# A hybrid layer: state-space outputs on quarter tiles, modulations moved into the state-space stage, TensorE order pinned there

## The chip, the core and the metric

The kernel runs on one core of a Trainium2 chip. The metric is the device time of one execution, in microseconds (us). A core has a matrix engine, TensorE (PE in the profile, its weight loads PEld), and VectorE (DVE), ScalarE (ACT) and GpSimd (POOL) beside it; SyncE (SP) only issues DMAs here, and its queue is in order. PSUM, where matmuls write, has eight banks of 128 partitions x 512 numbers of four bytes.

## The reference

One layer over 512 latent tokens with 256 context tokens in front, width 1024: an adaptive norm, one input projection, then two branches (a bidirectional state-space scan with 32 groups of 64 complex states, and attention with 8 query heads on 2 key heads), merged by gates, and a gated FFN with a short convolution. The modulations (shift, scale and gate vectors from `c`) are a vector times a 1024 x 6144 matrix.

```python
def _modulate(h, shift, scale):
    return h * (1.0 + scale) + shift
...
def _s5_readout(s_re, s_im, c_re, c_im):
    y = (jnp.einsum('blgn,gpn->blgp', s_re, c_re.astype(jnp.float32))
         - jnp.einsum('blgn,gpn->blgp', s_im, c_im.astype(jnp.float32)))
    return y.reshape(y.shape[0], y.shape[1], SSM_DIM)
...
    y_lat = u_lat.astype(jnp.float32) * d
    for direction in range(N_DIRECTIONS):
        sl_re, sl_im, sc_re, sc_im = _s5_direction(
            uc, ul, lam_re[direction], lam_im[direction], log_dt[direction],
            b_re[direction], b_im[direction], reverse=(direction == 1))
        y_lat = y_lat + _s5_readout(sl_re, sl_im, c_re[direction], c_im[direction])
...
def _merge_branches(attn_tok, ssm_tok, g, w_attn_br, w_glu, w_out):
    p_attn = attn_tok @ w_attn_br
    glu_a, glu_b = jnp.split(jax.nn.gelu(ssm_tok) @ w_glu, 2, axis=-1)
    p_ssm = glu_a * jax.nn.sigmoid(glu_b)
    g_attn, g_ssm = jnp.split(g, N_BRANCHES, axis=-1)
    return (jax.nn.sigmoid(g_attn) * p_attn + jax.nn.sigmoid(g_ssm) * p_ssm) @ w_out
...
        mod = jax.nn.silu(c) @ w_mod[layer] + b_mod[layer]
        sh1, sc1, g1, sh2, sc2, g2 = jnp.split(mod[:, None, :], N_MOD, axis=-1)
        h = _modulate(_rmsnorm(x, norm1_w[layer]), sh1, sc1)
        q, k, v, u, g = jnp.split(h @ w_in_l, (Q_END, K_END, V_END, U_END), axis=-1)
        attn_tok = _tokens(_gqa_sweep(q, jnp.concatenate([kc, k], axis=2),
                                      jnp.concatenate([vc, v], axis=2)))
        y_ssm, y_ssm_c = _s5_bidirectional(...)
        x_mix = _merge_branches(attn_tok, y_ssm, g, w_attn_br[layer], w_glu[layer], w_out[layer])
        x = x + g1 * x_mix
        h2 = _modulate(_rmsnorm(x, norm2_w[layer]), sh2, sc2)
        x = x + g2 * _conv_ffn(h2, w_up[layer], conv_w[layer], conv_b[layer], w_down[layer])
    return _rmsnorm(x, final_norm_w)
```

## The kernel before

All arithmetic is in four-byte numbers. A large product is made of three PE passes: operands are split into a high and a low part, and `mm3` (L127) adds high x high, low x high, high x low. `weight` (L136) loads a weight tile in pieces of 128x512 (`wr`, three buffers), ScalarE casts the high part `wh` (L133) and GpSimd subtracts for the low part `wl` (L134); both have two buffers. The stages, in us of the profiled execution:

- 0 to 82: norms, the modulations that the first norm needs (`wmA`), and the projection u for the scan, which goes to DRAM by block (`ud`, L418).
- 82 to 112: keys; lag matrices of block 0 (`s5_lags`, L462) and its tables (`turn`, L484).
- 112.5 to 286: the state-space stage, four blocks `s` of eight groups each in two halves `h`. `s5_build` makes W and H of a block with twelve DVE operations; `s5_lags` multiplies them on PE into `kps`, and turns the result through DRAM (`ldr`) into `tp`; `s5_drive` (L498) transposes W (`gps`) and multiplies it with u into two banks `gp`, of which it uses columns 0 to 4 x 96 of 512; `s5_half` (L521) multiplies by tables and scans on DVE, and then makes the outputs `y2` on PE: per group one full matmul with `tp` and u (L125) and four on 64 rows of the array with H and the states `q1` (L558), each streaming 64 columns. `s5_end` (L561) copies y2 and turns it through DRAM: one issue to `yd`, eight back into `y`. Beside this run v (`values_all`, six tiles `vp`) and twelve gate tiles (`gate_tile`, tiles `proj`, tanh on ACT): `beside(i)` writes them between the halves.
- 286 to 318: the gelu of y, and the first queries and scores. 318 to 500: the head loop, eight heads of four query blocks each: scores `sc`, softmax on DVE and ACT, transposes `tps` of P, value matmuls `po`, and between these, as filler, matmuls of the query two heads on (`query`) or of a gate, and of `glu`. In this loop stand the 16 remaining modulations, two per head (at j 0 and 3; turned at j 1 and 4): `mods_load` (L685) asks for one 1 MB tile `wm`, `mods_row` (L690) multiplies it with `c` on 32 columns of the array at a time, ScalarE copies the row to `tg` (L694), `mods_turn` (L697) turns it with two one-column matmuls and DVE adds the bias.
- 500 to 605: both branches' output projections. 605 to 990: the FFN, `up` and `down`.

PSUM banks come by tag: `a` and `b` two banks each, `s` two pairs. `vp`, `proj` in the stage, and `mods` have tag `a`; `gps` and `kps` have `b`; `gp`, `y2` and `sc` have `s`. What sets the order: in the head loop it is that of the code (`pinned`, L120: each matmul of `mm` is tied to the one before it). In the state-space stage it is not tied, and a scheduler chooses among what is written there. A `f32` matmul that is not of the split kind is two records in the profile: the eight of a modulation row are x16.

## Time and profile before

| | us |
|---|---|
| median of 3 runs | 993.87 |
| lowest and highest | 991.27, 996.55 |
| the profiled execution | 992.33 |
| its span in the profile | 990.3 |
| PE busy | 927.7 |
| state-space stage (112.5 to 286), PE busy in it | 173.5, 158.93 |
| head loop (318 to 500), PE busy in it | 182.0, 181.37 |

The span runs from the first to the last instruction; the execution's own time has some 2 us around it. A matmul's record overlaps the next one's, so a mean duration is longer than the distance from one to the next; the chain of work that ended last gives the distance. The windows give the clock that was granted to PE as a share of 2.4 GHz, as a mean over the stretch.

### The profile page before, as it was taken

How to read it: one execution, taken by the hardware profiler on the slowest of the kernel's cores; microseconds unless marked ns; L12 is line 12 of the kernel's file. 1: busy time of each engine (PE TensorE's matmuls, PEld its weight loads, DVE VectorE, ACT ScalarE, POOL GpSimd, SP SyncE). 2: the span in 40 equal slices, each digit the busy share in tenths (PEclk: the TensorE clock that was granted, in tenths of full speed). 3: DMA queues.
4: the chain of work that ended last, by engine and by line, in shares of the span. 5: the costliest groups of instructions: out<-in, count | busy, mean ns of one | idle time of the engine just before them, and what ended most of it. 6: DMA issues, size and time to landing. Idle time of an engine off the chain costs nothing.

```text
span 990.3 us, 14447 instructions
## 1 busy us (share of the span) xinstructions
PE 927.7 (94%) x5522; PEld 762.1 (77%) x5522; DVE 500.1 (51%) x957; ACT 406.0 (41%) x749; POOL 370.9 (37%) x282
## 2 busy tenths in 40 slices
PE   3978987999998999999999999999999999999996
PEld 1757776787886787777778898888888888888886
DVE  8497595769666666667433564423233332300103
ACT  7325432343264444444432343534443444432322
POOL 2242131532331221122235430655656555544553
PEclk9999998988999999999999999999999999999998
DMA  9516314151343233333313530232222323233332
GB/s 367 221 58 193 75 49 123 49 144 49 99 136 107 103 113 126 128 128 124 110 65 128 189 111 1 85 103 89 97 96 87 104 86 103 85 101 96 96 106 85
DMA packets 59443, 109.25 MB, mean 110 GB/s; under 512 B 10608, under 2 KB 23664, under 8 KB 55664
## 3 DMA queue, kind: packets, MB, share of 16 engines
q1 hardware_dynamic: 59376, 108.35, 33.6%
q8 instruction: 43, 0.70, 0.3%
q14 instruction: 24, 0.20, 0.1%
HBM read 102.06 MB, written 6.26 MB: 109 GB/s over the span
## 4 chain that ended last, share of the span: by engine, by line
PE 76%; DVE 8%; issue 4%; DMA 4%; POOL 3%; ACT 3%; SPq 2%; DVEq 0%; ACTq 0%; POOLq 0%
PE up L125 25%; PE down L125 12%; PE proj L125 10%; PE po L125 6%; PE glu L125 5%; PE sc L125 3%; PE pab L125 3%; POOL wl L134 3%; PE tps L805 2%; DMA wr<-wo 2%; PE mods L366 2%; PE y L558 1%; PE gp L517 1%; PE kp L125 1%; DVE tg L228 1%
## 5 line engine op out<-in xcount | busy, mean ns | idle before, releaser
L134 POOL TENSOR_TENSOR wl<-wr,wh 128x512 fp32r<-128x512 f32 x226 | 318.7, 1430 | 576.3 <-ACT wh L133 565.8
L125 PE MATMUL up<-t,wh 128*128 128x512 f32 (+1 forms) x768 | 225.5, 377 | 1.6 <-DVE t L933 0.9
L133 ACT CAST wh<-wr 128x512 fp32r<-128x512 f32 x226 | 127.8, 609 | 131.0 <-PE down L125 40.5
L125 PEld LDWEIGHTS up<-t,wh 128*128 128x128 f32 x768 | 140.0, 188 | 32.0 <-DVE t L933 2.4
L125 PE MATMUL up<-t,wl 128*128 128x512 f32 (+1 forms) x384 | 144.7, 377 | 0.0
L125 PE MATMUL proj<-h,wh 128*128 128x512 f32 x384 | 130.6, 408 | 3.0 <-DVE g L134 2.1
L125 PEld LDWEIGHTS proj<-h,wh 128*128 128x128 f32 x384 | 74.3, 194 | 17.9 <-ACT g L133 2.2
L125 PEld LDWEIGHTS up<-t,wl 128*128 128x128 f32 x384 | 72.2, 188 | 14.7
L125 PE MATMUL proj<-h,wl 128*128 128x512 f32 x192 | 78.1, 407 | 2.5 <-POOL wl L134 2.5
L967 DVE SCALAR_TENSOR_TENSOR zc<-up,pv,zc 128x511 f32<-128x511 f32 x44 | 33.0, 750 | 88.3 <-ACT zc L966 88.3
L966 ACT ACTIVATE zc<-up,pv 128x512 f32<-128x512 f32 x44 | 34.2, 777 | 74.9 <-PE up L125 74.9
L998 DVE SCALAR_TENSOR_TENSOR x<-down,mods,x 128x512 f32<-128x512 f32 (+1 forms) x9 | 6.2, 691 | 90.7 <-PE down L125 90.7
L125 PEld LDWEIGHTS proj<-h,wl 128*128 128x128 f32 x192 | 37.4, 195 | 10.0 <-POOL wl L134 3.1
L125 PE MATMUL glu<-w,wh 128*128 128x512 f32 x128 | 44.2, 406 | 0.0
L134 DVE TENSOR_TENSOR ptl<-tps,pth 128x512 fp32r<-128x512 f32 x48 | 33.1, 689 | 16.6 <-ACT pth L133 16.1
L133 ACT CAST pth<-tps 128x512 fp32r<-128x512 f32 x48 | 28.2, 587 | 32.1 <-PE tps L805 32.1
L793 DVE TENSOR_REDUCE sc<-sc 128x1 f32<-128x768 f32 x32 | 30.7, 961 | 19.7 <-PE sc L125 19.7
L125 PE MATMUL sc<-g,qh 128*128 128x256 f32 (+1 forms) x128 | 37.6, 347 | 0.0
L125 PE MATMUL down<-h,wh 128*128 128x512 f32 x112 | 35.6, 389 | 0.0
L968 DVE SCALAR_TENSOR_TENSOR zc<-up,pv,zc 128x511 f32<-128x511 f32 x44 | 33.0, 750 | 1.5
L106 ACT ACTIVATE P<-sc,nb,rq 128x768 f32<-128x768 f32 x32 | 31.7, 993 | 4.8 <-DVE nb L794 3.1
L125 PE MATMUL po<-pth,g 128*128 128x512 f32 x96 | 32.4, 418 | 0.6 <-ACT pth L133 0.6
(286 smaller groups left out, 1763.3 us busy)
## 6 DMA issues: line engine op xcount, KB each, us to landing
wr<-wup SPq DMA_DIRECT2D x88, 256.0 KB
wm<-wmB SPq DMA_DIRECT2D x16, 1024.0 KB
wr<-wdn SPq DMA_DIRECT2D x40, 256.0 KB
x<-x SPq DMA_DIRECT2D x4, 1024.0 KB
g<-wmA SPq DMA_DIRECT2D x4, 1024.0 KB
w<-wmA SPq DMA_DIRECT2D x4, 1024.0 KB
wr<-wgs SPq DMA_DIRECT2D x16, 256.0 KB
wr<-wga SPq DMA_DIRECT2D x16, 256.0 KB
```

What stands on the lines that cost most here:

```text
L106: i = A.activation(*a, **k).ins
L125: pe(T.matmul(ps, l, r, start=start, stop=stop).ins)
L133: A.copy(hi, src)
L134: eng.tensor_tensor(lo, src, f(hi), op=OP.subtract)
L228: eng.tensor_tensor(o, a, b, op=op)
L366: pe(T.matmul(ps[c:c + 32, 0:n], l, r, start=j < 4, stop=j >= len(terms) - 4, tile_position=(0, c)).ins)
L517: T.matmul(gp[64 * g:64 * g + 64, ri, o:o + NC], gt[:, 2 * d + ri, 64 * g:64 * g + 64], u[:, 2 * k + g, c], start=True, stop=True, tile_po ...
L793: V.tensor_reduce(mx, sv, axis=AX.X, op=OP.max)
L805: pe(T.transpose(tps[:, 128 * b:128 * b + 128], Ps[h][b][:, 128 * j:128 * j + 128], ident).ins)
L966: A.activation(z, ps, AF.Identity, scale=cw[1], bias=pv[:, PV_CB + i:PV_CB + i + 1])
L967: V.scalar_tensor_tensor(z[:, 1:512], ps[:, 0:511], cw[0], z[:, 1:512], op0=OP.mult, op1=OP.add)
L968: V.scalar_tensor_tensor(z[:, 0:511], ps[:, 1:512], cw[2], z[:, 0:511], op0=OP.mult, op1=OP.add)
```

## The change

- The outputs of a half block are made after the scans by `s5_out`: u and the states `q1` are now the stationary operands and `tp` and H stream, 128 columns each; every matmul of the states uses a quarter of the array (64 rows x 64 columns), the one with u a half (64 columns). A pair of halves (k2, g) goes to partitions 64 x (g xor k2) of bank k2; they write into columns 384 to 512 of the `gp` banks of the same half's drive, which the drive leaves free. So `y2` is gone.
- `s5_end` turns y on PE against the identity (16 matmuls a block, quarter tiles) in a bank `yt` of tag `b`; the way through DRAM is gone. u is written to DRAM in an order in which one DMA per block (`s5_u`) reads it, eight before. On the host, columns of `w_u` and rows of `w_glu` are put in the matching order.
- All 16 modulations leave the head loop. They are made in the stage, each as two half rows (`wm` of 512 KB, two buffers); the row's copy goes to a buffer `bb`, and the bias is added by two ScalarE activations.
- PE's order in the stage is pinned. Generators yield after pieces of a few matmuls, and `weave(one, two, n, m)` takes n steps of the one with m of the other spread between them. `filler` is the list of six v tiles, twelve gates and, between their steps, the modulations; `steps(fill, ..)`, `GAP` and F0 to F3 say how much of it goes where.
- The low part of v is subtracted from a second copy `vr` that ScalarE makes, not from the bank. The tiles `p` have two buffers, three before, and z shares the one of p2.

```diff
+GAP, F0, F1, F2, F3, WM = 2, 8, 13, 5, 2, 2
...
     def s5_u(s):
-        u = tz([8, NC + NL], "u", 2)
-        for t in range(TC):
-            S.dma_start(u[16 * t:16 * t + 16], us_[s][:, t].rearrange("(j q) c -> q j c", j=8))
-        return u
-
+        us[s] = tz([8, NC + NL], "u", 2)
+        S.dma_start(us[s], us_[s].rearrange("t (q j) c -> (t q) j c", j=8))
...
+    def weave(one, two, n, m):
+
+        j = 0
+        for i in range(n):
+            next(one, None)
+            while j * n < (i + 1) * m:
+                next(two, None)
+                j += 1
+        run(one)
...
-        blocks[s] = W, H, tp, s5_u(s)
+        blocks[s] = W, H, tp, us[s]
...
+        for _ in range(GAP):
+            next(fill, None)
+            yield
...
         tt(q1[:, 0], q1[:, 0], q2[:, 1], OP.add)
         tt(q1[:, 1], q1[:, 1], q2[:, 0], OP.subtract)
-        for k2 in range(2):
-            k = 2 * h + k2
-            o = slice(NL * k, NL * k + NL)
-            for g in range(2):
-                mm(y2[:, g, o], tp[:, 2 * k + g], u[:, 2 * k + g, NC:NC + NL], True, False)
-            for d in range(2):
-                for ri in range(2):
-                    for g in range(2):
-                        pa = slice(64 * g, 64 * g + 64)
-                        T.matmul(y2[:, g, o], H[pa, ri, 2 * k + d], q1[pa, ri, 2 * k2 + d], start=False,
-                                 stop=d + ri == 2, tile_position=(64 * g, 0))
-
-    def s5_end(s, y2):
-        ys = t2()
-        A.copy(ys.rearrange("p (k g c) -> p g k c", k=4, g=2), y2[:, :, 0:4 * NL].rearrange("p g (k c) -> p g k c", k=4))
-        yd = dram.tile([128, 8, NL], F32, tag="yd", name="yd", bufs=4)
-        S.dma_start(yd, ys.rearrange("p (j c) -> p j c", j=8))
+        outs[s, h] = q1
+        yield
+
+    def s5_out(s, h, ys):
+
+        W, H, tp, u = blocks[s]
+        gp, q1 = drives.pop((s, h)), outs.pop((s, h))
+        four = [(k2, g, 2 * h + k2, slice(64 * (g ^ k2), 64 * (g ^ k2) + 64)) for k2 in range(2) for g in range(2)]
+        o = slice(4 * NC, 512)
+        for k2, g, k, px in four:
+            pe(T.matmul(gp[px, k2, o], u[:, 2 * k + g, NC:NC + NL], tp[:, 2 * k + g], start=True, stop=False,
+                        tile_position=(0, px.start)).ins)
+        for d in range(2):
+            for ri in range(2):
+                for k2, g, k, px in four:
+                    pa = slice(64 * g, 64 * g + 64)
+                    pe(T.matmul(gp[px, k2, o], q1[pa, ri, 2 * k2 + d], H[pa, ri, 2 * k + d], start=False, stop=d + ri == 2,
+                                tile_position=(64 * g, px.start)).ins)
+        A.copy(ys.rearrange("p (t b k l) -> p b k t l", t=TC, b=2, k=2)[:, :, h],
+               gp[:, :, o].rearrange("p b (t l) -> p b t l", t=TC))
+
+    def s5_end(s, ys):
+
+        yt = bank("yt", "b")
         for t in range(TC):
-            S.dma_start(y[:, s, NL * t:NL * t + NL], yd[16 * t:16 * t + 16].rearrange("p j c -> j p c"))
-
-    s5_build(0)
+            for px in (slice(0, 64), slice(64, 128)):
+                pe(T.matmul(yt[px, NL * t:NL * t + NL], ys[px, 64 * t:64 * t + 64], ident[px, px],
+                            start=True, stop=True, tile_position=(px.start, px.start)).ins)
+        A.copy(y[:, s], yt)
+
+    run(s5_build(0))
...
+    def v_tile(j, w):
+        ps = bank("vp")[:, :256]
+        for k in range(KT):
+            if j < 2:
+                st_ = (ch[:, k, 128 * j:128 * j + 128], cl[:, k, 128 * j:128 * j + 128])
+            else:
+                st_ = (hh[k][:, 128 * j - 256:128 * j - 128], hl[k][:, 128 * j - 256:128 * j - 128])
+            mm3(ps, st_, (w[k // 4][0][:, k % 4], w[k // 4][1][:, k % 4]), k == 0, k == KT - 1)
+            if k == KT - 1:
+                A.copy(vh[:, j], ps)
+                raw = tz([256], "vr")
+                A.copy(raw, ps)
+                V.tensor_tensor(vl[:, j], raw, f(vh[:, j]), op=OP.subtract)
+            if k % 2:
+                yield
+
+    ms, ga = [], []
+
+    def gate_w(i):
+        return weight(io["wgs" if i < 8 else "wga"][i % 8], [KT, 128])
+
+    def gate_of(o, w, tag):
+
+        ps = bank("proj", tag)
+        for k in range(KT):
+            mm3(ps, (w[0][:, k], w[1][:, k]), (hh[k], hl[k]), k == 0, k == KT - 1)
+            if k == KT - 1:
+                act(o, ps, AF.Tanh, scale=0.5)
+            yield
+
+
+    mods = tl([4, KT], "mods")
+    pieces = []
+
+    def mods_load():
+        p = len(pieces)
+        if p < 32:
+            wm = tz([4, 256], "wm", WM)
+            nosync(S.dma_start(wm, io["wmB"][p // 2, :, 4 * (p % 2):4 * (p % 2) + 4]).ins, last[0])
+            pieces.append(wm)
+
+    def mods_all():
+
+        yield
+        for i in range(16):
+            ps = bank("mods")
+            for p in range(2):
+                wm = pieces[2 * i + p]
+                for j in range(4):
+                    pe(T.matmul(ps[32 * j:32 * j + 32, 0:256], cz[:, 4 * p + j], wm[:, j], start=p == 0, stop=p == 1,
+                                tile_position=(0, 32 * j)).ins)
+                mods_load()
+                if p == 0:
+                    yield
+            row = tz([256], "bb", 2)
+            A.copy(row, ps[:, 0:256])
+            yield
+            for t in range(2):
+                mm(ps[:, 256 + t:257 + t], row[:, 128 * t:128 * t + 128], sel[:, 0:1], True, True)
+            o = PV_BMOD + 16 + 2 * i
+            for t in range(2):
+                acts["run"].append(A.activation(mods.rearrange("p v k -> p (v k)")[:, 2 * i + t:2 * i + t + 1],
+                                                ps[:, 256 + t:257 + t], AF.Identity, bias=pv[:, o + t:o + t + 1]).ins)
+            yield
+
+    def filler():
+        mod = mods_all()
         wv_ = [weight(io["wv"][i], [4, 256]) for i in range(2)]
+        jobs = [("v", j) for j in range(6)] + [("g", i) for i in range(8 + NGA)]
+        w = wv_
+        for n, (kind, i) in enumerate(jobs):
+            if kind == "v":
+                gen = v_tile(i, wv_)
+            else:
+                if i == 0:
+                    ms.extend(rows("x8", F32))
+                if i == 8:
+                    ga.extend(rows("c8", F32))
+                gen = gate_of((ms + ga)[i], w, "a")
+            if n + 1 < len(jobs) and jobs[n + 1][0] == "g":
+                w = gate_w(jobs[n + 1][1])
+            m = 0
+            for _ in gen:
+                m += 1
+                yield
+                if n < 16 and m in ((1, 2, 4) if kind == "v" else (2, 5, 8)):
+                    next(mod, None)
+        for _ in mod:
+            yield
...
+    fill = filler()
+    for _ in range(WM):
+        mods_load()
+    pinned[0] = True
+    run(s5_drive(0, 0))
+    for s in range(4):
+        ys = t2()
+        if s < 3:
+            s5_u(s + 1)
+
+        weave(s5_half(s, 0), chain(s5_drive(s, 1), fill), 8, 6 + F0)
+        s5_out(s, 0, ys)
+        if s < 3:
+            weave(chain(turn(2 * s + 2), s5_build(s + 1)), fill, 15, F1)
+            weave(chain(s5_half(s, 1), turn(2 * s + 3)), chain(s5_drive(s + 1, 0), s5_lags(s + 1), fill), 8, 9 + F2)
         else:
+            weave(s5_half(s, 1), fill, 8, F0)
+        s5_out(s, 1, ys)
+        steps(fill, F3)
+        s5_end(s, ys)
+    run(fill)
+    pinned[0] = False
...
-            if j in (1, 4):
-                mods_turn(*turning)
             if j < 4 and h + 1 < HEADS:
                 scores(h + 1, j)
-            if j in (0, 3):
-                turning = mods_row(*wm)
-                if wm[0] < 15:
-                    wm = mods_load(wm[0] + 1)
...
```

TensorE, the outputs of a half block. Rows are line, operation, out<-in and shape; the numbers behind `h` tell apart the buffers of the norm's output. Before (`y` is the pair of banks y2):

```order
L125 MATMUL proj<-h_265,wh 128x512
L125 MATMUL proj<-h_264,wh 128x512
L125 MATMUL proj<-h_264,wl 128x512
L558 MATMUL y_1550<-tg,w_1304 128x64 x8
L125 MATMUL y_1550<-u,tp 128x64 x2
L558 MATMUL y_1550<-tg,w_1304 128x64 x8
L125 MATMUL y_1550<-u,tp 128x64 x2
L125 MATMUL proj<-h_266,wh 128x512
```

And now:

```order
L127 MATMUL proj<-h_263,wl 128x512
L127 MATMUL proj<-h_265,wh 128x512
L596 MATMUL gp<-tp,u 64x128 x4
L602 MATMUL gp<-w_1299,tg 64x128 x16
L127 MATMUL proj<-h_264,wh 128x512
L127 MATMUL proj<-h_264,wl 128x512
L127 MATMUL proj<-h_266,wh 128x512
L726 MATMUL mods<-wm,cz 32x256 x4
```

The group has 20 matmuls as before, of 128 columns each and not 64, and the half row of a modulation stands close by.

TensorE, the step from one gate tile to the next (the first rows are the end of a tile, where `h_264` and `h_266` are used; a tile begins with `h_263`). Before:

```order
L125 MATMUL proj<-h_264,wh 128x512
L125 MATMUL proj<-h_264,wl 128x512
L125 MATMUL proj<-h_266,wh 128x512
L125 MATMUL proj<-h_263,wh 128x512
L125 MATMUL proj<-h_263,wl 128x512
```

And now:

```order
L127 MATMUL proj<-h_264,wl 128x512
L127 MATMUL proj<-h_266,wh 128x512
L726 MATMUL mods<-wm,cz 32x256 x4
L127 MATMUL proj<-h_263,wh 128x512
L127 MATMUL proj<-h_263,wl 128x512
L127 MATMUL proj<-h_265,wh 128x512
L127 MATMUL proj<-h_263,wh 128x512
L127 MATMUL proj<-h_263,wl 128x512
L127 MATMUL proj<-h_265,wh 128x512
L127 MATMUL mods<-cst,bb 128x1 x2
```

The second half row of a modulation stands between two gate tiles, and its bank, opened some steps earlier with the same tag `a`, is held across the step until the turn and the two activations behind it.

SyncE's queue, around the weights of the last gates in the stage (`wgs` and `wga`). Before:

```order
L425 DMA u<-ud 16x8x160 x5
L450 DMA bb<-sc 128x256
L565 DMA yd<-tg 128x512
L425 DMA u<-ud 16x8x160
L478 DMA ldr<-lg 128x240
L425 DMA u<-ud 16x8x160
L567 DMA y_719<-yd 128x1x64 x8
L481 DMA tp<-ldr 16x8x128 x8
L425 DMA u<-ud 16x8x160
L145 DMA wr<-wga 128x512 x6
```

And now:

```order
L147 DMA wr<-wgs 128x512 x2
L499 DMA ldr<-lg 128x240
L715 DMA wm<-wmB 128x1024
L502 DMA tp<-ldr 16x8x128 x8
L715 DMA wm<-wmB 128x1024
L428 DMA u<-ud 128x1280
L147 DMA wr<-wgs 128x512
L147 DMA wr<-wga 128x512
L715 DMA wm<-wmB 128x1024 x2
L468 DMA bb<-sb 128x256
L147 DMA wr<-wga 128x512
L469 DMA bb<-sc 128x256
```

The small issues of y and u are gone from between the weights, and loads of `wm` and of the next block's `bb` stand there.

## Rows read from the trace of the kernel before

**Rows 1.** The page's part 1: busy time of each engine, share of the span, instructions.

```profile
PE 927.7 (94%) x5522; PEld 762.1 (77%) x5522; DVE 500.1 (51%) x957; ACT 406.0 (41%) x749; POOL 370.9 (37%) x282
```

**Rows 2.** Busy time by stretch: the state-space stage, the head loop.

```profile
core 0: us, PE busy (x) PEld busy (x) DVE busy (x) ACT busy (x) POOL busy (x), PEclk, DMA share, GB/s
112.50:286.00 173.50, 158.93 (x1290) 133.54 (x1290) 127.21 (x215) 64.82 (x125) 55.40 (x33) 0.93 0.29 83
318.00:500.00 182.00, 181.37 (x1110) 143.35 (x1113) 117.22 (x277) 83.80 (x163) 37.78 (x28) 1.00 0.35 122
```

**Rows 3.** The same view in windows of 3 us around long waits.

```profile
99.00:102.00 3.00, 1.66 (x26) 1.66 (x26) 0.00 (x0) 0.59 (x1) 0.00 (x0) 0.82 1.08 240
102.00:105.00 3.00, 3.00 (x14) 1.85 (x12) 0.00 (x0) 1.19 (x3) 0.00 (x0) 0.61 1.16 167
165.00:168.00 3.00, 0.00 (x0) 0.00 (x0) 3.00 (x9) 0.00 (x0) 0.00 (x0) 0.63 0.70 182
201.00:204.00 3.00, 3.00 (x54) 2.77 (x57) 0.90 (x1) 2.94 (x6) 1.33 (x2) 0.50 0.78 232
204.00:207.00 3.00, 3.00 (x53) 2.45 (x45) 0.79 (x2) 1.26 (x3) 0.00 (x0) 0.54 0.81 173
```

**Rows 4.** PE's timeline: start, us, instruction, in brackets idle time before and releaser.

```profile
100.34 0.97 PE L517 MATMUL gp<-u,gt 128*64 128x96 f32 x15 [4.07 <-DMA wr<-wv]
...
112.57 0.50 PE L125 MATMUL vp<-wh,c 128*128 128x256 f32 x2 [0.78 <-ACT tg L106]
...
137.87 0.47 PE L125 MATMUL proj<-h,wh 128*128 128x512 f32 x1 [2.12 <-DVE g L134]
...
168.37 0.87 PE L125 MATMUL y<-u,tp 128*128 128x64 f32 x3 [6.28 <-DMA wr<-wgs]
...
198.35 0.50 PE L125 MATMUL proj<-h,wl 128*128 128x512 f32 x1 [2.29 <-POOL wl L134]
```

**Rows 5.** The timeline of SP's DMA issues: start, us that the issues took.

```profile
95.02 1.88 SPq L425 DMA_DIRECT2D u<-ud  x3
...
155.42 5.08 SPq L567 DMA_DIRECT2D y<-yd  x8
...
162.38 3.62 SPq L481 DMA_DIRECT2D tp<-ldr  x8
166.10 0.85 SPq L145 DMA_DIRECT2D wr<-wgs  x2
```

**Rows 6.** The chain of work that ended last, head loop: start, us, instructions.

```profile
317.96 1.00 PE mods L366 x16
...
323.07 0.34 PE mods L125 x4
...
327.56 1.76 PE po L125 x6
...
354.11 1.76 PE po L125 x6
```

**Rows 7.** PE's timeline where scores go over into a modulation.

```profile
332.48 0.28 PE L125 MATMUL sc<-g,ql 128*128 128x256 f32 x1
332.60 0.28 PE L125 MATMUL sc<-g,qh 128*128 128x256 f32 x1
332.81 1.07 PE L366 MATMUL mods<-wm,cz 128*32 128x256 f32 x16
```

**Rows 8.** ACT's groups: shape and count, busy us, mean ns, idle before and releaser.

```profile
L694 ACT COPY tg<-mods 128x256 f32<-128x256 f32 x16 | 6.0, 373 | 43.3 <-PE mods L366 43.3
L106 ACT ACTIVATE x<-proj 128x512 f32<-128x512 f32 x8 | 4.7, 593 | 20.8 <-PE proj L125 20.8
L133 ACT CAST g<-vp 128x256 fp32r<-128x256 f32 x6 | 2.2, 368 | 2.6 <-PE vp L125 2.4
```

**Rows 9.** A load of wm: its issue, and windows of 0.5 us behind it.

```profile
307.36 0.33 SPq L687 DMA_DIRECT2D wm<-wmB  x1
...
309.50:310.00 0.50, 0.50 (x4) 0.42 (x3) 0.50 (x2) 0.00 (x0) 0.00 (x0) 1.00 1.04 442
311.50:312.00 0.50, 0.50 (x5) 0.45 (x4) 0.00 (x0) 0.00 (x0) 0.00 (x0) 1.00 0.17 49
312.00:312.50 0.50, 0.50 (x7) 0.50 (x6) 0.28 (x1) 0.00 (x0) 0.00 (x0) 1.00 0.00 0
```

**Rows 10.** The chain of work that ended last, state-space stage.

```profile
176.50 1.47 PE gp L517 x32
...
246.04 1.04 PE y L558 x16
247.08 0.59 PE y L125 x4
```

**Rows 11.** The lag matmuls: one stretch of PE's timeline, and the tile's durations (min/median/max).

```profile
149.54 0.57 PE L472 MATMUL kps<-w,wpad 128*32 128x112 f32 x14
...
L472 PE MATMUL kps<-w,wpad x128: 259/259/394, 81.7 to 241.7; 128*32 128x112 f32 x128
```

**Rows 12.** GpSimd's timeline: three subtractions.

```profile
190.84 10.22 POOL L134 TENSOR_TENSOR wl<-wr,wh 128x512 fp32r<-128x512 f32 x3 [5.37 <-ACT wh L133]
```

More of the change, by code (lines that the diff above doesn't have):

```diff
@@ L2 @@
 from contextlib import ExitStack
+from itertools import chain
 import concourse.bass as bass
@@ L431, in hybrid_layer_kernel @@
     G.memset(wpad, 0.0)
[L432 removed]
+    blocks, tabs, drives, outs = {}, {}, {}, {}
     def built(o, src, scal, s):
@@ L451, in s5_build @@
         W, H = k8("k12", [2, 8, 128]), k8("w8", [2, 8, 128])
-        built(W, bb, ws, s)
+        blocks[s] = W, H, cb_
+        yield from built(W, bb, ws, s)
         for g in range(2):
@@ L458, in s5_build @@
                 A.activation(dst, src, AF.Copy, scale=-1.0 if ri else 1.0)
-        built(H, cb_, hs, s)
-        blocks[s] = W, H, cb_
+        yield from built(H, cb_, hs, s)
     def s5_lags(s):
@@ L617, in keys @@
         table("silu_and_others")
+    s5_u(0)
     keys()
[L620 to L637 removed]
@@ L677, in hybrid_layer_kernel, with steps @@
-    for i in todo:
-        gate_tile(i)
+    run(s5_lags(0))
+    run(turn(0))
+    run(turn(1))
+    def steps(gen, n):
+        for _ in range(n):
+            next(gen, None)
+    def v_tile(j, w):
[12 more added lines that the diff above has]
+            if k % 2:
+                yield
@@ L770, in gate @@
     def gate(i, w):
-        ps = bank("proj", "b")
-        for k in range(KT):
-            mm3(ps, (w[0][:, k], w[1][:, k]), (hh[k], hl[k]), k == 0, k == KT - 1)
-            if k == KT - 1:
-                act(ga[i], ps, AF.Tanh, scale=0.5)
-            yield
+        return gate_of(ga[i], w, "b")
     def scores(h, b):
@@ L813, in values @@
         mm3(po, (vh[:, j, vs], vl[:, j, vs]), pt, j == 0, j == 5)
-    def steps(gen, n):
-        for _ in range(n):
-            next(gen, None)
     qs, Ps, sums = {}, {}, {}
```

132 lines of the change are left out of this document (47 added, 85 removed).

## Prediction

> **What bounds the kernel now.** I read the page first: TensorE (PE) is busy 927.7 of 990.3 us [rows 1], so a gain has to come out of what PE does or waits for. Then the stretches by stage [rows 2]. In the head loop of attention (318 to 500 us) PE is busy 181.37 of 182.00 us at full clock: what is taken off PE there shortens the program one to one, as long as nothing else becomes late. In the state-space stage (first v matmul at 112.5 us to the query norms at 286) PE is busy 158.93 of 173.5 us and its mean granted clock is 0.93. So 14.6 us are idle, and the low clock costs up to 0.07 x 173.5 = 12.1 us, some 1.1 of it while PE was idle anyway (63% granted in 3 us without any work, [rows 3]): 25.6 us of losses and 147.9 us of work at full speed. VectorE (DVE) is busy 127.21 us there, ScalarE (ACT) 64.82: neither fills the stage, but both hand PE its operands.
>
> Then I read who ends PE's waits [rows 4] and what the clock does behind them [rows 3]. Four waits carry most of it: 4.07 us before the first drive, 2.12 us at the step from v to the gates, 6.28 us at 162 to 168 us, 2.29 us at 196 us. After each long one the clock stands at its lower level (0.50 of 2.4 GHz is 1.2 GHz) for some us; behind the 2.29 us wait the two windows from 201 to 207 us lose 1.5 + 1.4 = 2.9 us more. The first and third waits end with a DMA (the profile names the last one to land; the drive itself reads u), and SyncE's (SP's) queue shows why: eight issues of y<-yd take 5.08 us, eight of tp<-ldr 3.62, and only then the gate weights go out at 166.10 us [rows 5].
>
> **The change part by part.** The sum is made against the profiled execution's own 992.33 us.
>
> *Modulations out of the head loop.* All 16 move, each with 16 PE matmul instructions for the row (1.00 us on the chain) and 4 to turn it (0.34 us) [rows 6]. 16 x 1.34 = 21.4 us, all on the path. With less between them the transposes of P and the value matmuls could meet their ACT and DVE work sooner; in each place query or glu matmuls remain between, so I take the whole: **-21.4**. The 16 loads of 1 MB leave that loop's queue too; nothing waited for them.
>
> *Modulations into the stage.* They return as 32 half rows of 8 instructions. A half is 0.50 us by [rows 6], and each is entered from another tile shape. That costs some 0.1 us: of two like score matmuls the second starts 0.12 us after the first, and the modulation behind them 0.21 after that [rows 7]. 32 x 0.60 + 16 x 0.34 = **+24.6** of PE work. Their DVE addition goes to ACT, where 32 small activations and 16 copies of 0.37 us [rows 8] sit in idle time. Loads: 1 MB was issued at 307.36 us and its last bytes moved by 312.0, 4.6 us for 1 MB [rows 9]; the stage asks for 1 MB per v tile (24 matmuls and one modulation, some 4.3 us) at first and per gate (some 7.5 us) later. In the v part that is just enough, so up to 0.5 us a tile, 3 us in all, may be waited; later nothing.
>
> *Outputs on quarter tiles.* Before, a half block costs 2 x (1.04 + 0.59) = 3.26 us [rows 10], 26.1 us for eight. After, it has 8 instructions with u stationary and 32 with the states stationary, each streaming 128 columns. No row shows a 64x64 tile. Nearest is gp: 32 in 1.47 us, 46 ns for 96 columns with two column tiles [rows 10], 61 ns for 128. Below that lies kps with four column tiles at a time: 14 in 0.57 us of which one lasts 0.26 [rows 11], so 24 ns for 112 columns, 27 for 128. Above it lies 65 ns for 64 columns (1.04 us for 16), 130 for 128, if nothing overlaps. I take 61, since two column halves are sure. 40 x 61 ns = 2.45 us a half, 19.6 for eight. The turn of y by PE, 32 instructions of 64 columns a block, is 31 ns each by gp, 3.9 us for four blocks (8.3 at 65 ns). Together -26.1 + 19.6 + 3.9 = **-2.6**; the ends are -11.3 (27 ns) and +19.4 (130 and 65 ns).
>
> The rows of y show two row halves that write to different banks, each 65 ns. The new code lets both row halves of a pair write to one bank. The Trainium skill, "TensorEngine Tiling (Array Packing)", section "Gotcha 1: PSUM Pressure", says that different row tiles cannot access one PSUM bank at the same time; by it the pairs of a bank would not overlap, the upper end. No row of before shows two row tiles on one bank, so this is a rival below.
>
> *SP's queue.* Gone are 32 issues of y<-yd, 4 of yd, and 28 of the 32 of u<-ud: at 0.63 us for y and u (5.08 / 8 and 1.88 / 3, [rows 5]) that is some 38 us of the queue. 16 issues more of wm, 0.33 us each [rows 9], come in. Each wm load waits until PE has used the buffer, and gate weights, bb and tp are queued behind it; the order has the weights of a gate a tile ahead, so this costs nothing while PE runs, and a gate's delay would pass on to the next. With the queue free the 4.07 us wait for u goes, and the clock lost behind it, 0.18 x 3 + 0.39 x 3 = 1.7 us [rows 3]: **-5.8** before the first v matmul.
>
> *Waits in the stage.* Of the 25.6 us lost I expect to keep the step from v to gates (2.12 us, and 1.5 us of clock), since both weight buffers are still held by v. New is this: a modulation's bank now stands between two proj tiles, so a proj tile takes the bank of the one just before it, and PE waits for ACT to empty it: 0.59 us for a gate's tanh, twice 0.37 for v [rows 8] plus some 0.3 us to start, against the half row of 0.6 us. I put 0.4 us at 17 boundaries, 6.8 us. The order is pinned, so one wait of PE on DVE or on GpSimd (whose subtractions of 1.4 us stretched to 10.22 for three while DVE worked, [rows 12]) will remain somewhere: 2.29 + 2.9 + 0.5 = 5.7 us as at 196 us. In all 16.1 us instead of 25.6: **-9.5**. The work of gp and of v, gates, lags is the same. PE's work grows to about 172 us, DVE's stays near 127, so DVE is late only locally, in a block's 12 build operations.
>
> Sum: -21.4 + 24.6 - 2.6 - 5.8 - 9.5 = -14.7, so 977.6 us; the median of the runs stands 1.5 us above the profiled execution (993.87 to 992.33), so **979 us**.
>
> **The rivals.** (a) *Four quarters at a time and no long wait.* 27 ns for the outputs (-8.7) and no wait on DVE or GpSimd (-5.7), some boundary waits hidden (-3): 962. For it: four column tiles do overlap in kps. Against: a long in-order chain of four engines seldom has no late link.
>
> (b) *The quarter tiles run one after the other*, slower than before: two row tiles on one bank, 130 ns a matmul in the outputs and 65 in the turn, +22.0 on the forecast: 1001. Place: the eight output groups. It passes before's 993.87 + 0.5% from about 121 ns a matmul on. For it: 65 ns for 64 columns today is no sign of overlap. Against: each pair also has different columns of the array, as gp has, and gp overlaps. This is the case that the skill's sentence above would give.
>
> (c) *The pinned order stalls.* Eight outputs and three builds stand on PE's queue with filler of fixed length; where DVE is late, nothing may pass. Each such wait costs 5.7 us as at 196 us; five more than the one I count give 979 + 28 = 1007, and four already decide. For it: DVE has 127 us of work in a stage that becomes no longer, and slow GpSimd beside it. Against: DVE's share is 127 of about 188.
>
> (d) *The change does not do what it says in attention*: the loop hands back half of the 21.4 us because value matmuls wait for P: 990. Against: DVE has 117.22 and ACT 83.80 of 182 us there [rows 2].
>
> **How the numbers follow.** Forecast 0.50 (its own range 969 to 988: +-9 from the boundary waits and the wm loads), (a) 0.20, (b) 0.11, (c) 0.12, (d) 0.07. A measurement of this kernel can tell about 0.5%, 5 us, from no change. Faster than that: the forecast, (a) and a part of (d), 0.73; within it: the rest of (d) and the good edges of (b) and (c), 0.11; slower 0.16. The range for 8 in 10 takes in (a) and the near part of (b): 957 to 1000.
>
> **What would show it.** In the new profile the head loop's period (between two first groups of value matmuls, 354.11 - 327.56 = 26.6 us, [rows 6]) falls to about 23.9 us with PE still full (if not, (d)). A group of outputs takes about 2.4 us; 1.4 is (a), 4.6 is (b). Between two proj tiles PE waits about 0.4 us with ACT as releaser; waits of over 2 us with DVE as releaser in front of an output, and a granted clock near 0.5 behind, are (c). The first v matmul starts near 106 us. The stage from there to the query norms lasts about 185 us. The forecast is wrong if PE's quarter tiles or the waits for wm are far from these prices.

## The result and the profile after

The changed kernel takes 979.89 us (median of 4 runs, 977.92 to 985.58) against 993.51 us of the kernel before (4 runs): 0.987 of its time, 95% interval 0.9821 to 0.9919. The forecast was 979. The profiled execution took 977.92 us, its span is 976.0, 14.3 us less than before. The total was right; the terms of its sum were off by 2.6 to 6.7 us each, with both signs, as the sections below show. The traces are of one execution of each kernel, for the changed one the fastest of the four.

The page's part 1, busy time of each engine:

```profile
PE 920.3 (94%) x5650; PEld 742.6 (76%) x5650; DVE 494.8 (51%) x941; ACT 416.4 (43%) x795; POOL 361.2 (37%) x282
```

The span falls into three pieces at two marks that both kernels have: the first v matmul, and the first place in the chain where six value matmuls stand together, `po` x6 (the loop's first value matmuls come in threes, 16 to 18 us earlier). Before, these stand at 112.57 and 327.56 us [rows 4, 6]. The windows between the marks, of the changed kernel and then of the kernel before:

```profile
104.20:337.14 232.94, 215.43 (x1957) 161.49 (x1958) 156.87 (x289) 102.41 (x227) 60.84 (x40) 0.97 0.43 131
```

```profile
112.57:327.56 214.99, 197.65 (x1505) 164.91 (x1506) 154.31 (x285) 87.09 (x165) 63.36 (x40) 0.94 0.30 92
```

So the stretch ahead of v is 8.4 us shorter, the middle 17.95 us longer, the rest of the program 23.9 us shorter (662.7 to 638.9). In the runs below whose code behind the second mark is the same, this rest takes 639.2 to 643.3 us, so differences of 2 us between single traces say little. The chain of work that ended last, of the changed kernel; the first two rows are one group of outputs, the third a turn of y, then the head loop:

```profile
159.11 0.59 PE gp L596 x8
159.70 1.03 PE gp L602 x32
162.89 1.10 PE yt L612 x32
...
329.26 2.75 PE glu L127 x12
...
333.14 2.77 PE glu L127 x12
...
337.14 1.76 PE po L127 x6
...
360.39 1.77 PE po L127 x6
```

The outputs of a half block take 0.59 + 1.03 = 1.62 us (2.45 forecast, 3.26 before, [rows 10]): 32 ns for one matmul record of a quarter tile. The head loop's period is 360.39 - 337.14 = 23.25 us, 3.30 less than before [rows 6]; 2.7 was forecast.

PE's timeline, the start of v and the longest waits of the stage (idle time and releaser in brackets):

```profile
104.20 0.50 PE L127 MATMUL vp<-wh,c 128*128 128x256 f32 x2 [0.78 <-ACT tg L108]
...
134.38 1.01 PE L127 MATMUL mods<-cst,bb 128*128 128x1 f32 x4 [3.41 <-ACT bb L732]
...
189.60 0.64 PE L726 MATMUL mods<-wm,cz 128*32 128x256 f32 x8 [2.83 <-ACT mods L738]
...
234.29 0.64 PE L726 MATMUL mods<-wm,cz 128*32 128x256 f32 x8 [2.57 <-ACT mods L738]
```

PE's waits that ended with a DMA before [rows 4] are gone, and three others have come. Behind the first, in windows of 3 us, the granted clock (last but two) falls to its lower level, 0.50 of 2.4 GHz, which costs some 2.9 us more (1.5 + 1.05 in the second and third window, and half of the 0.62 us that PE works in the first):

```profile
132.00:135.00 3.00, 0.62 (x3) 0.62 (x4) 3.00 (x4) 0.37 (x1) 0.00 (x0) 0.71 0.21 79
135.00:138.00 3.00, 3.00 (x17) 1.97 (x18) 3.00 (x5) 0.75 (x4) 0.00 (x0) 0.50 0.02 5
138.00:141.00 3.00, 3.00 (x20) 2.46 (x20) 3.00 (x4) 0.72 (x3) 0.00 (x0) 0.65 0.51 175
...
234.00:237.00 3.00, 2.71 (x15) 1.87 (x16) 3.00 (x5) 0.86 (x4) 0.00 (x0) 0.78 0.38 113
237.00:240.00 3.00, 3.00 (x15) 1.43 (x14) 3.00 (x5) 1.52 (x3) 0.23 (x1) 0.65 0.19 75
```

Behind the third it costs 1.7 us (the last two rows, 0.22 x 2.71 + 0.35 x 3); behind the second the clock stays up. DVE is busy for all of these 15 us. ScalarE is named as releaser; what it waited for itself is in the timelines of ACT, DVE and GpSimd:

```profile
133.95 0.37 ACT L732 COPY bb<-mods 128x256 f32<-128x256 f32 x1 [4.01 <-issue]
...
188.50 0.63 ACT L478 ACTIVATE wpad<-k 64x128 f32<-64x128 f32 x2 [4.66 <-DVE k L230]
189.14 0.41 ACT L738 ACTIVATE mods<-mods,pv 128x1 f32<-128x1 f32 x2
```

```profile
129.24 1.23 DVE L230 TENSOR_TENSOR k<-bb,ws 128x1024 f32<-128x1024 f32 x1 [3.15 <-DMA bb<-sb]
...
132.66 1.22 DVE L230 TENSOR_TENSOR t<-bb,ws 128x1024 f32<-128x1024 f32 x1
133.79 2.35 DVE L230 TENSOR_TENSOR w<-bb,hs 128x1024 f32<-128x1024 f32 x2
...
182.81 3.44 DVE L230 TENSOR_TENSOR w<-bb,hs 128x1024 f32<-128x1024 f32 x2
186.17 2.30 DVE L230 TENSOR_TENSOR k<-k,t 128x1024 f32<-128x1024 f32 x1
...
189.73 1.21 DVE L230 TENSOR_TENSOR k<-k,t 128x1024 f32<-128x1024 f32 x1
```

```profile
183.12 4.26 POOL L136 TENSOR_TENSOR wl<-wr,wh 128x512 fp32r<-128x512 f32 x2 [7.01 <-ACT wh L135]
```

The row copy at 133.95 begins when DVE has read bb for the last time (132.66 + 1.22 = 133.88): the row shares the two buffers of that tag with the next block's data. At 188.50 the copies into `wpad` stand at the head of ScalarE's queue, waiting for DVE's W (`k`); the two activations that free a modulation's bank stand behind them. At the second and third place DVE loses time because its operations take longer while GpSimd subtracts: two of `w` take 3.44 us where two take 2.35 without GpSimd (at 133.79), and one of `k` 2.30 where it takes 1.21. The Trainium skill, "SBUF — State Buffer", section "Who interferes with whom", says that a DVE instruction with two SBUF inputs contends with a GpSimd instruction that reads SBUF. By these rows the trace agrees: DVE lost (3.44 - 2.35) + (2.30 - 1.21) = 2.2 us in GpSimd's 4.26.

GpSimd is not all of it: at the first place it is idle (0.00 in the windows from 132 to 141 us). There DVE begins the build late, after 3.15 us of waiting for the load of bb (129.24), and the builds of blocks 2 and 3 begin with such a wait too (4.58 and 1.84 us). SP's queue and the chain of work show where it comes from:

```profile
109.01 16.38 SPq L715 DMA_DIRECT2D wm<-wmB  x6
125.48 0.38 SPq L468 DMA_DIRECT2D bb<-sb  x1
```

```profile
173.41 4.83 DMA bb<-sb
...
218.38 4.54 DMA bb<-sb
```

The load of bb is issued behind loads of wm, each of which waits until PE has used a buffer; at the two later places the chain of work that ended last leads through the load of bb, the build on DVE, the copies into wpad and the bank of the modulation to PE. No run moved these loads alone, so what they cost by themselves is not shown; e1_row and e11_rowpin below come nearest to it.

### The profile page after: what moved, and what is told of

Read it like the earlier page. It is cut to its first block, busy times and chain, and to the rows that moved or that the text cites. A ratio compares the mean times of both kernels' runs of the same rounds, so it can differ in the third digit from the quotient of the medians.

```text
span 976.0 us, 14672 instructions
## 1 busy us (share of the span) xinstructions
PE 920.3 (94%) x5650; PEld 742.6 (76%) x5650; DVE 494.8 (51%) x941; ACT 416.4 (43%) x795; POOL 361.2 (37%) x282
## 4 chain that ended last, share of the span: by engine, by line
PE 78%; DMA 6%; DVE 6%; issue 5%; ACT 3%; POOL 1%; SPq 0%; DVEq 0%; ACTq 0%; POOLq 0%
PE up L127 25%; PE down L127 12%; PE proj L127 11%; PE po L127 6%; PE glu L127 5%; PE sc L127 3%; PE pab L127 3%; PE tps L889 2%; DMA wr<-wo 2%; PE ul L127 2%; DVE k L230 2%; DMA g<-wmA 1%; DMA bb<-sb 1%; PE kp L127 1%; DVE w L230 1%
## 5 line engine op out<-in xcount | busy, mean ns | idle before, releaser
L136 POOL TENSOR_TENSOR wl<-wr,wh 128x512 fp32r<-128x512 f32 x226 | 309.0, 1387 | 571.3 <-ACT wh L135 554.2
L127 PE MATMUL proj<-h,wh 128*128 128x512 f32 x384 | 140.4, 416 | 2.2 <-ACT c L108 0.7
L127 PE MATMUL proj<-h,wl 128*128 128x512 f32 x192 | 76.1, 396 | 0.0
L136 DVE TENSOR_TENSOR h<-tg,h 128x512 fp32r<-128x512 f32 x16 | 14.8, 925 | 35.8 <-ACT h L135 35.8
```

The lines of the kernel that those rows point to most:

```text
L127: pe(T.matmul(ps, l, r, start=start, stop=stop).ins)
L136: eng.tensor_tensor(lo, src, f(hi), op=OP.subtract)
```

## The experiments

The runs go after two questions: what the modulations and the quarter tiles were each worth, and what makes the stage's waits. The medians are those of 3 rounds; each ratio is to the kernel before on the same chip. "Stage" is the length between the two marks (232.94 us in the changed kernel, 214.99 before).

**The modulations back in the head loop (e4_home).**

```diff
+            if j in (1, 4):
+                mods_turn(*turning)
...
+            if j in (0, 3):
+                turning = mods_row(*wm)
...
-                if n < 16 and m in ((1, 2, 4) if kind == "v" else (2, 5, 8)):
-                    next(mod, None)
```

> The 16 modulations go back into the head loop as they were in the kernel before (row on TensorE at j 0 and 3, turn at 1 and 4, addition on DVE, 1 MB loads); all the rest of the change stays. By the prediction's prices (21.4 us in the head loop, 24.6 us in the stage, waits that are not the modulations'): 977 us. Theory (the modulations bring the stage's waits: 26.8 us of their own work, 8.8 us of waits, 5.1 us of clock, against 26 to 28 us in attention): 965 to 968 us. Rival (the waits are DVE's and stay, each side costs the same): 979 to 982 us.

992.4 us, 0.9995 (0.9971 to 1.0018): all of the gain is gone, and none of the three cases had that. The first v matmul stands at 108.84 us, the stage takes 218.43, the head loop's period is 353.82 - 327.27 = 26.55 us again. PE's timeline, some of its waits:

```profile
142.16 0.80 PE L127 MATMUL proj<-h,wl 128*128 128x512 f32 x1 [3.31 <-POOL wl L136]
...
189.00 2.83 PE L547 MATMUL gp<-u,gt 128*64 128x96 f32 x32 [4.13 <-ACT gt L535]
```

PE is idle for 28.1 us of the stage (all bracketed waits between the marks together), against 16.3 with the modulations in it and 17.3 before. So without filler PE runs ahead of the gates' weights (cast, then GpSimd's subtraction) and of the drive. Two things follow. A modulation that goes into the stage costs less than its PE time: the changed kernel's stage is 14.5 us longer than this one, which still has two modulations of its own (3.3 us), so the 16 cost some 17.8 us. And, in this pinned order, what the quarter tiles save turns into waits unless something fills the stage; the stage without both the modulations and the pinned order was not tried.

**Two quarters at a time (e5_diag), and each row half its own bank (e6_bankg).**

In e5_diag the column half is the row half:

```diff
-        four = [(k2, g, 2 * h + k2, slice(64 * (g ^ k2), 64 * (g ^ k2) + 64)) for k2 in range(2) for g in range(2)]
+        four = [(k2, g, 2 * h + k2, slice(64 * g, 64 * g + 64)) for k2 in range(2) for g in range(2)]
```

In e6_bankg the column half is k2, and the bank is the row half (in both matmuls; one is shown):

```diff
-        four = [(k2, g, 2 * h + k2, slice(64 * (g ^ k2), 64 * (g ^ k2) + 64)) for k2 in range(2) for g in range(2)]
+        four = [(k2, g, 2 * h + k2, slice(64 * k2, 64 * k2 + 64)) for k2 in range(2) for g in range(2)]
...
-                pe(T.matmul(gp[px, k2, o], q1[pa, ri, 2 * k2 + d], H[pa, ri, 2 * k + d], start=False, stop=d + ri == 2,
+                pe(T.matmul(gp[px, g, o], q1[pa, ri, 2 * k2 + d], H[pa, ri, 2 * k + d], start=False, stop=d + ri == 2,
```

> The outputs' quarter tiles stand only on the diagonal of the array: row half g always with column half g (both pairs), so that two of them can run side by side and not four; the channels come out in another order, which the host's order of the rows of w_glu follows. Theory 1 (four quarters run at a time: 32 ns each in the changed kernel): two at a time cost 53 to 64 ns each, 0.7 to 1.0 us a group, 5 to 8 us of TensorE work in all. If that lies on the path: 985 to 988 us; if the waits of the stage take it up: 981 to 983 us. Theory 2 (32 ns is set by issue, not by the array): the group stays at 1.0 us and the time at 980 us.

> The outputs of row half g go to bank g and columns half k2, so that the two row halves never write to the same bank; the channels come out in another order, which the host follows. If two row halves on one bank hold each other up in the changed kernel: the group of 32 falls from 1.03 us to 0.85 us or less and the time to some 978 us. If sharing a bank costs nothing: 1.03 us a group and 980 us.

The chain of work, one group of e5_diag and one of e6_bankg:

```profile
162.71 1.89 PE gp L602 x32
```

```profile
161.28 1.03 PE gp L602 x32
```

With two at a time the group takes 1.89 us, 59 ns a record against 32: more than two quarters do run side by side. The time is 990.84 us, 0.9995 (0.997 to 1.0019), the stage 243.85: 10.9 us longer for 8 x 0.86 = 6.9 us of work. The time is above all that was said (985 to 988). PE's idle time does not explain the rest, it hardly changes (18.1 us to 17.5 between the marks): two waits for `wl` (4.9 us) stand where those for a modulation's bank stood. The clock explains most of it: in windows of 1 us PE loses 9.3 us of its busy time to it, 6.3 in the changed kernel. Here, where the modulations fill the stage, the outputs lie on the path. With a bank for each row half nothing changes: 980.37 us, 0.9868. The sentence of the Trainium skill on row tiles and PSUM banks ("TensorEngine Tiling (Array Packing)", "Gotcha 1: PSUM Pressure"), on which the second rival stood, does not show in the time of these tiles, whose row halves write to different partitions of the bank: 1.03 us with a shared bank, 1.03 without.

**The row's buffer and wpad's copies (e1_row, e2_wpad, e3_both).**

The first hunk is e1_row, the second e2_wpad; e3_both has both:

```diff
-            row = tz([256], "bb", 2)
+            row = tz([256], "row")
...
-                A.activation(dst, src, AF.Copy, scale=-1.0 if ri else 1.0)
+                V.tensor_scalar(dst, src, -1.0 if ri else 1.0, None, op0=OP.mult)
```

> The row of a modulation gets a buffer of its own (tag row, one buffer) and no longer shares the two of bb with the data of the next block's build. Theory (shared buffer): the 3.41 us wait of TensorE in the last v tiles, which ends when DVE has read bb for the last time, goes, and with it the 3.4 us that the low clock costs in the 9 us behind it; the two later waits of 2.83 and 2.57 us stay. About 973 us. Rival (DVE is late in itself): the wait moves to the next operand of the block's build and the time stays within 978 to 982 us.

> The four small copies into wpad of each block go from ScalarE to DVE, which makes their source. Theory (ScalarE's queue): wpad's copies wait for DVE at the head of ScalarE's queue and hold up the modulation's two activations behind them, and TensorE waits for the bank; so the waits of 2.83 and 2.57 us go, with 1.7 us of clock behind the second: about 974 us; the 3.41 us wait stays. Rival (DVE is late in itself): TensorE waits as long for the lag matmuls or the transposes of W, and DVE has 16 operations more: 980 to 984 us.

> Both edits together. If both theories hold the gains add: 979.9 - 6.8 - 7.1, about 966 to 968 us, and no wait of TensorE over 1 us is left between the first v matmul and the last gate. If DVE is late in itself: 978 to 984 us.

985.8 us (0.9926), 987.08 (0.9944), 987.0 (0.994): each slower than the changed kernel by its median, though the intervals (from 0.9895 up, against 0.9919 at most) still touch, and each above all that was said. In e1_row the 3.41 us wait is gone, and the two later ones have grown. PE's timeline:

```profile
185.12 0.79 PE L127 MATMUL proj<-h,wh 128*128 128x512 f32 x1 [4.76 <-ACT x L108]
...
233.88 0.80 PE L127 MATMUL proj<-h,wh 128*128 128x512 f32 x1 [4.83 <-ACT x L108]
```

ACT's timeline ahead of the first of them, and DVE's:

```profile
181.34 0.62 ACT L511 ACTIVATE t<-t,cc 128x384 f32<-128x384 f32 x1 [4.84 <-DVE t L230]
...
184.50 0.57 ACT L108 ACTIVATE x<-proj 128x512 f32<-128x512 f32 x1
```

```profile
176.68 4.18 DVE L572 TENSOR_TENSOR_SCAN p<-sp,p 128x96 f32<-128x96 f32 x8
```

Now the table of the next half (L511) stands at the head of ScalarE's queue and waits for DVE, whose eight scans take 4.18 us while GpSimd works (2.10 otherwise); a gate's tanh stands behind it, and PE needs that gate's bank. The stage is 232.44 us long, hardly shorter than with the wait (232.94). The first v matmul slips to 109.73 us, because the free buffers let the build of block 1 move ahead among the keys. In e2_wpad the stage is 238.52 us: PE waits for DVE itself at the lag matmuls, and for a copy of the outputs:

```profile
196.10 0.40 PE L491 MATMUL kps<-w,wpad 128*32 128x112 f32 x8 [2.55 <-DVE w L230]
...
210.62 1.96 PE L612 MATMUL yt<-cst,tg 64*64 64x64 f32 x32 [2.76 <-ACT tg L604]
```

With both edits the two later waits are 5.26 and 5.49 us. Both theories of a single place fell: what is taken away at one place of ScalarE's queue stands at the next, as long as DVE is late.

**The buffer again, without the move of the build (e11_rowpin).**

```diff
-        S.dma_start(bb, io["sb"][s])
-        S.dma_start(cb_, io["sc"][s])
+        for t, name in ((bb, "sb"), (cb_, "sc")):
+            i = S.dma_start(t, io[name][s]).ins
+            if pinned[0]:
+                nosync(i, last[0])
...
-            row = tz([256], "bb", 2)
+            row = tz([256], "row")
```

> As the run with a buffer of its own for the row, and the loads of bb are tied to the place in TensorE's order where the build is written, so that the build of block 1 can not move ahead of the keys. Theory (the 3.41 us wait is the shared buffer, and the first run lost its gain because the builds moved): first v matmul near 104 us, no wait in the v tiles, clock up: 973 to 975 us. Rival (the wait passes to the next ScalarE instruction that waits for DVE, as after the first edit): first v near 104 us, but the waits of the gates grow to 4 to 5 us each: 978 to 981 us.

979.66 us (0.9863), the first v at 105.20, the stage 234.51. The wait in the v tiles is 2.12 us in place of 3.41, now for v's second copy, which DVE reads, and the gates wait 2.78 and 1.84 (4 to 5 each were said). The rival's time held: the shared buffer is where the wait shows, not why it is there. DVE waits 3.29 us for the load of bb here too, while in e1_row the load for block 1 went out at 65.22 us, ahead of the loads of wm, and PE had no such wait left in the v tiles. So the late build makes the first wait, and not the buffer alone. The later waits of e1_row came although its builds waited for no load.

**DVE with less to do (e9_noh), GpSimd with less to do (e10_nosub).**

The first two hunks are e9_noh, the last is e10_nosub:

```diff
-        W, H = k8("k12", [2, 8, 128]), k8("w8", [2, 8, 128])
+        W, H = k8("k12", [2, 8, 128]), blocks[0][1] if s else k8("w8", [2, 8, 128])
...
-        yield from built(H, cb_, hs, s)
+        if s == 0:
+            yield from built(H, cb_, hs, s)
+        else:
+            for _ in range(6):
+                yield
...
-        return weight(io["wgs" if i < 8 else "wga"][i % 8], [KT, 128])
+        src, h = io["wgs" if i < 8 else "wga"][i % 8], tl([KT, 128], "wh", 2, F32R)
+        for k in range(0, KT, 4):
+            r = tl([4, 128], "wr", WR)
+            S.dma_start(r, src[:, k:k + 4])
+            A.copy(h[:, k:k + 4], r)
+        return h, h
```

> The H matrices of blocks 1 to 3 are not built; those of block 0 are used in their place, so 18 of the 36 operations of DVE in the stage's three builds (1.2 to 2.3 us each, some 25 us) are left out of the computation; TensorE's work is the same. Theory (DVE is late, and ScalarE's queue passes it on): the three waits of 3.41, 2.83 and 2.57 us shrink to under 1 us each, and the clock stays up behind them: 966 to 970 us. Rival (the loads of wm or the banks hold TensorE): the waits stay, 977 to 981 us.

> The twelve gates of the stage use the high part of the weights in place of the low part: GpSimd's 24 subtractions there are left out, TensorE's matmuls stay. Theory (GpSimd's subtractions slow DVE down, 2.30 us for 1.21 of the same operation, and so make it late): DVE's busy time in the stage falls by 8 us or more, the waits of 2.83 and 2.57 us go: 971 to 974 us. Rival (DVE's late work is its own order, behind loads): 978 to 981 us.

e9_noh: 977.27 us (0.9832); DVE's busy time between the marks falls from 156.87 to 129.12 us, yet the stage only to 229.68. The 3.41 us wait is still there (3.65), the others are 1.58 and 1.40. So it is not DVE's total that counts: the build of block 1 still begins after 3.40 us of waiting for bb. e10_nosub: 973.04 us (0.9797, 0.975 to 0.9843), the stage 225.76, the later waits gone or 0.53 us. The first wait stays, at 3.40 us: GpSimd did not make it. The windows between the marks:

```profile
103.10:328.86 225.76, 213.71 (x1957) 160.61 (x1958) 144.25 (x289) 102.59 (x227) 19.31 (x16) 0.98 0.43 135
```

DVE does the same operations as in the changed kernel in 12.6 us less (144.25 to 156.87): that is about what GpSimd's 24 subtractions took from it.

**The subtractions on DVE (e12_dvewl), and with e11's edits (e13_all).**

```diff
-        return weight(io["wgs" if i < 8 else "wga"][i % 8], [KT, 128])
+        return weight(io["wgs" if i < 8 else "wga"][i % 8], [KT, 128], V)
```

> The low parts of the twelve gates' weights are subtracted on DVE (24 x 0.69 us = 16.6 us) and not on GpSimd. Theory (GpSimd's work slows DVE by about as much as it would take DVE itself): DVE's busy time from the first v to the first value group of attention stays near 157 us, the two waits of 2.8 and 2.6 us shrink: 973 to 977 us. Rival (DVE has no room for it): new waits for wl with DVE as releaser, 984 us or more.

> Both edits: row with its own buffer and bb loads tied to TensorE's order, and the gates' low parts on DVE. If both theories hold the gains add: 967 to 971 us. If DVE has no room: 978 us or more.

975.86 us (0.982, 0.9779 to 0.9861) and 974.93 (0.9815, 0.9777 to 0.9852). In e12_dvewl the waits of 2.83 and 2.57 us are gone, the stage is 227.41 us, 5.5 less, and DVE is busy hardly longer for its 24 operations more. The first wait stays. The windows between the marks, DVE's timeline at the place shown above, and the first wait:

```profile
106.03:333.44 227.41, 215.77 (x1957) 162.02 (x1958) 158.43 (x313) 103.02 (x227) 19.27 (x16) 0.97 0.42 134
```

```profile
185.07 1.22 DVE L230 TENSOR_TENSOR k<-k,t 128x1024 f32<-128x1024 f32 x1
...
188.69 1.28 DVE L136 TENSOR_TENSOR wl<-wr,wh 128x512 fp32r<-128x512 f32 x2
```

```profile
136.30 0.94 PE L127 MATMUL mods<-cst,bb 128*128 128x1 f32 x4 [3.51 <-ACT bb L732]
```

`k` takes 1.22 us, not 2.30, and a subtraction 0.64, not the 2.1 that GpSimd needed beside DVE. The theory of e12 held. The gain of both edits together did not add (967 to 971 expected): on top of e12's edit the buffer is worth 0.9 us, within the noise, since the first wait is still there in e13_all, 2.10 us at v's second copy.

**The order not pinned (e8_unpin).**

```diff
     for _ in range(WM):
         mods_load()
-    pinned[0] = True
     run(s5_drive(0, 0))
```

> The order of TensorE in the state-space stage is not pinned; all else as in the changed kernel, the scheduler chooses. If the pinned order itself makes the waits (the prediction's third rival): fewer waits, 970 to 975 us. If the pinned order is what keeps filler in the places where the block waits: gates, v and modulations run ahead of the blocks and the end of the stage is left without filler: 985 to 995 us.

975.44 us (0.9824, 0.9777 to 0.9871). The six value matmuls of the second mark stand at 332.04 us, 5.1 earlier than in the changed kernel, though the first v comes later (109.52, other work goes ahead of it). PE is idle for 10.6 us from the first v on. Its timeline, a wait for DVE:

```profile
186.96 0.44 PE L533 MATMUL gps<-cst,k 128*128 128x128 f32 x2 [0.88 <-DVE k L230]
```

DVE is late for `k` here too, but PE has passed the gates in the meantime. So it takes the pinned order to turn most of DVE's lateness into lost time, and either end of that is worth about 4 us by the medians; which of the pinned places it is was not tried, nor this together with e13's edits. The intervals of e8 to e13 all overlap that of the changed kernel (0.9821 to 0.9919); the stage's lengths and the waits in the traces are what tells them apart. The lowest median of a kernel here that computes the whole layer is that of e13_all, 974.93 us, 0.9815 of before.

## Why the prediction was right, and where it was not

The terms of the sum against the two traces, in us (the fifth is read from windows, the sixth is what remains of the stage's +17.95):

| term | forecast | measured |
|---|---|---|
| ahead of the first v | -5.8 | -8.4 |
| modulations out of the head loop | -21.4 | -26.4 |
| modulations into the stage (PE) | +24.6 | +31.3 |
| outputs on quarter tiles, turn of y | -2.6 | -8.7 |
| waits and clock in the stage | -9.5 | -5.9 |
| other PE work in the stage | 0 | +4.5 |
| sum | -14.7 | -13.6 (span -14.3) |

*Ahead of the first v.* The wait for u and the clock behind it went as forecast. Most of the rest is no gain: the first drive, 32 records of 1.47 us [rows 10], stood ahead of the first v before [rows 4] and stands behind it now (at 105.82 us).

*Modulations out.* Right in kind, 5 us too small. 16 x 3.30 / 2 = 26.4. The step that failed is the price of 1.34 us each: it took the modulation's own pieces of the chain, and not what they did to the next one. The glu group behind a row took 2.98 us and takes 2.75 now, that behind a turn 2.92 and now 2.77, the transposes behind the other row 0.59 and now 0.44. These in the chain of the kernel before:

```profile
318.96 2.98 PE glu L125 x12
...
323.41 2.92 PE glu L125 x12
...
333.88 0.59 PE tps L805 x4
```

*Modulations in.* The same mistake with the other sign. PE's timeline around a half row in the changed kernel:

```profile
126.78 0.28 PE L127 MATMUL vp<-wl,h 128*128 128x256 f32 x1
126.99 0.64 PE L726 MATMUL mods<-wm,cz 128*32 128x256 f32 x8
127.56 0.51 PE L127 MATMUL vp<-wh,h 128*128 128x256 f32 x2
127.90 0.28 PE L127 MATMUL vp<-wl,h 128*128 128x256 f32 x1
128.02 0.40 PE L127 MATMUL vp<-wh,h 128*128 128x256 f32 x2
128.26 0.28 PE L127 MATMUL vp<-wl,h 128*128 128x256 f32 x1
```

From 126.78 it starts 0.21 us later where v's matmuls follow at 0.12; it lasts 0.57; the pair behind it takes 0.34 where the next pair takes 0.24. In all 0.09 + 0.57 + 0.10 = 0.76 us, where I had 0.60: I counted the way into the other shape and not the way out. 32 x 0.76 + 16 x 0.44 (a turn, read in the same way) = 31.3. e4_home bears it out: between the marks PE's work at full clock (busy time less what the clock took, in windows of 1 us) is 181.39 us there and 209.15 in the changed kernel, 27.8 more, where 31.3 less the 3.3 of e4's own two gives 28.0.

*Outputs.* The mechanism was right, the size was off: 8 x 1.62 + 4 x 1.10 = 17.4 us against 26.1. The step that failed is the choice of gp's 61 ns (two column halves) as the nearest row. With 32 ns the lower bound, kps with four tiles side by side (27 ns), was nearer; e5_diag measured the other case at 59 ns. So rival (a), with 27 ns, was nearer to the price, and rival (b) fell: a record takes 32 ns, not 130, and e6_bankg shows the bank to cost nothing. Two ends of the recorded sum are wrong, without touching the forecast: 320 records at 27 ns cost 8.6 us, which is 11.0 less than 19.6 and not 8.7, so the lower end was -13.6 and not -11.3; with the turn at 65 ns the upper end was +23.8 and not +19.4.

*Waits and clock.* Two thirds of this came, and by another way than forecast. PE's idle time between the marks, by the windows, which also count gaps too short for a bracket, is as long as before (232.94 - 215.43 = 17.5 us, 17.3 before); what the low clock took of its busy time fell from 12.3 to 6.3 us, in windows of 1 us. In place of the waits at tile boundaries, forecast at 6.8 us, stand 1.44 (v, for its second copy) and 0.69; in place of the step from v to the gates, at 2.12, stands 0.61. But there are three long waits, 8.8 us with 4.6 of clock behind two of them, where I had allowed one. The step that failed is that bb, queued behind the loads of wm, costs nothing, and that DVE, at 127 of 188 us, is late only in places. The loads of bb hold up the start of each of the three builds (3.15, 4.58 and 1.84 us), GpSimd's subtractions slow the second and third build, and in a pinned order each such place is paid. That is rival (c) in a smaller edition: e12 takes away the two later waits by way of GpSimd, e8 loosens the order. That the first wait comes from the load of bb is read from the traces (e1_row against e11_rowpin) and not tested by itself.

*Other PE work.* The sum had "the work of gp and of v, gates, lags is the same". It is not: PE's work at full clock rose from 185.31 to 209.15 us between the marks, by 23.8, where 31.3 - 2 x 1.65 (two modulations stood in this stretch before) - 8.7 gives 19.3. Of the 4.5 us between, 1.5 is the drive that moved behind the mark. The rest is not the modulations', since e4_home has it too (181.39 us, 3.9 less than before, where the outputs alone give 8.7); what it is was not tried.

*Rival (d)* was wrong: the head loop gave back nothing. e4_home shows more than it asked: without the modulations in the stage the rest of the change, in this pinned order, is worth nothing, since PE then waits 28.1 us for weights and drives.

The errors: -2.6, -5.0, +6.7, -6.1, +3.6 and +4.5 us. They cancel to 1.1, which is luck; the range would have held the time with any two of them alone, so the total is no proof of the steps.

## What to carry to other kernels

Price work that is put between other work by the start times of its neighbours on both sides, with and without it, not by its own rows. A stage in which one engine has slack takes filler cheaply and gives back little for faster work, as e4_home shows for this one; ask what its waits would be once either is changed alone. Where an in-order queue (ScalarE's here) evacuates banks and also waits for a slow producer, a single removed wait goes to the next instruction of that queue: look for what makes the producer late, its own loads in another queue included.

## What was not expected of the hardware

Quarter tiles of TensorE on all four quarters ran at 32 ns for 128 columns of f32, on two at 59; with all four it made no difference whether two row halves wrote to the same bank. DVE operations with two inputs from SBUF took 1.21 us alone and 2.30 beside GpSimd's subtractions, eight scans 2.10 and 4.18; moving 24 subtractions to DVE raised its busy time by 1.6 us in all (156.87 to 158.43).
